# Output projection's input rings for its first blocks, and the down pass's residual adds on VectorE with later norms

## The chip, the cores and the metric

The kernel runs on one core of a Trainium2 chip. The metric is the device time of one execution in microseconds (us), the median over several runs. Five engines work side by side, each through its own instructions in order: TensorE (PE, matmuls), VectorE (DVE), ScalarE (ACT), GpSimd (POOL) and SyncE (SP), which here issues most of the DMAs. They wait for each other by semaphores.

## The reference

One layer of an encoder, with the same weights for a prompt of 2048 tokens and a sample of 256; d is 1024, the feed-forward width is 2816.

```python
h = rmsnorm(x, norm1_w)
p = h @ w_in
mq, mk, mv, mo, gates, aq, ak, av = jnp.split(p, cuts, axis=-1)
m_out = mlstm_mixer(mq, mk, mv, mo, gates, b_gates, mh_norm_w)
a_out = attention_mixer(aq, ak, av, q_norm_w, k_norm_w)
x = x + jnp.concatenate([m_out, a_out], axis=-1) @ w_out
h = rmsnorm(x, norm2_w)
u = centred_dwconv(h @ w_up, conv_w, conv_b)
a, g = jnp.split(u, 2, axis=-1)
x = x + (jax.nn.silu(g) * a) @ w_down
return rmsnorm(x, final_norm_w)
```

All of it is float32. The kernel splits each operand into a high and a low part of a shorter format, and makes a product from three matmuls (high by high, high by low, low by high).

## The kernel before, in words

The 2304 tokens are worked on as columns. The phases, in order: input projection and norm; gates; attention side by side with the mLSTM (`run_both`, L1689); the output projection, `phase_c` (L999), begun when the mLSTM is through and woven into the rest of the attention; the up projection with convolution and silu; the down pass, which ends with the residual and the final norm.

**Who orders the work.** A scheduler puts the instructions of every engine in order as the kernel is built. Only PE, from the end of the mLSTM to the end of the attention, follows the order in which the code is written (L1707). There `run_both` takes one piece of attention and one piece of the output projection in turn; a piece of the latter is a chunk of 12 matmuls (a `yield` in `mm`, L1048).

**The output projection.** It goes over 9 blocks of 256 tokens (BT), in the order 0 to 6, 8, 7; `n` is the place in that order and `b` the block. A block has 8 input tiles `cmx` (128 of the 1024 mixed channels each), read from `mix_d`, and one tile `cx` of the residual input x. `loads(n, b)` (L1020) brings them in: per tile a DMA on SP (L1031), the high part by a copy on ACT (L1032) and the low part by a subtraction on DVE (L1033); then x (L1036). The tiles of a block live in one of two rings with room for exactly one block each:

- `mx` (MXB = 8), in the pool `c_s`, which is opened when the mLSTM's own pools are closed: its memory is free only when the mLSTM is through;
- `nT` (NTB = 8), in the pool `m_n`, the ring in which the mLSTM had its own inputs: it is free as soon as the last mLSTM projection has been made, earlier than `mx`.

A block's loads are called at the start of the block before it (L1089), so they wait, if for anything, for the last user of their ring. A block needs 4 outputs `z` of 2 x 128 channels, 48 matmuls each (L1045, into `po`), then the residual (DVE, L1052), a store (L1054), squares (ACT, L1056) and their sum (POOL, L1058). The weights `wo` come in two halves; the first (k = 0, for z = 0 and 1) is loaded early, the second (k = 1) has its stage in the pool `c_s`; L111 is its DMA, L112 its copy on ACT, L114 its subtraction on DVE.

**The down pass.** Strassen-like: 7 products (`DOPS`), of which each is made for 3 column blocks `z` of 384 tokens (CG), each of these over 11 pairs `p` of channel blocks, with 12 matmuls (L1531) each. That is 21 groups of 132 matmuls, one behind the other on PE. Activations `te`/`tet` come in pieces (L1416 on SP) and are split by ACT and DVE (L1373, L1374), as the weights `we`/`wet` are. After a group, `update` adds its result to the accumulators `c00`, `c01`, `c10`, `c11` (L1541 and, for the product t3, L1543 on DVE).

What else belongs to the end of the layer is called from a table: `at(n, f)` runs f behind the matmuls of step n, where n counts pairs p over all groups. `resid` (L1433) loads a residual tile `xe` (L1436 on SP) and adds it to an accumulator (L1438: 128 partitions x 1536 elements, 12 times). `squares` (L1444, ACT) and `collect` (L1450, L1453, POOL) make the sum of squares `sm`. `norm` (L1455) sums that over partitions (three small matmuls in the code, L1461, six in the profile), adds eps (DVE, L1464), takes the power -1/2 (POOL, L1465), spreads the result to all partitions by PE (three more, L146, six in the profile), scales 8 slices on DVE (L1469) and stores them (L1471, SP). `xe` and `qe` share a ring of 2 buffers ("x"), so a residual's load can wait until the squares of another accumulator have been collected.

The first three norms (hf = 0, z = 0 to 2) fall into the products t3 and t1. After t3's update of block z come the adds for `c10` and `c01`, the squares of `c10`, their collection, and then the norm of that block.

Of the kernel before, what the change touches and what calls it, by code (L numbers as in the profile page):

```python
# [12 lines left out]
ALU = mybir.AluOpType  # L13
# [79 lines left out]
def f32(ap):  # L93
    return ap.bitcast(F32)
# [48 lines left out]
def rstd_rows(g, ps, r, n):  # L143

    for t in range(n // P):
        g.nc.tensor.matmul(ps[:, t * P:(t + 1) * P], r[:, t:t + 1].to_broadcast([P, P]), g.ident, start=True, stop=True)  # L146
    return ps[:, 0:n]
# [851 lines left out]
def phase_c(g, sn, sp, pp, wps):  # L999
# [3 lines left out]
    nc = g.nc  # L1003
# [17 lines left out]
    def loads(n, b):  # L1021
        mx = []
        x = sp.tile([P, NCC, BT], F32, tag="x", name=f"cx{b}", bufs=2)
        for z in range(4):
            for o in range(2):
                c = 2 * z + o
                if n % 2 == 0:
                    m = sp.tile([P, 2, BT], F32R, tag="mx", name=f"cmx{b}_{c}", bufs=MXB)
                else:
                    m = sn.tile([P, 2, BT], F32R, tag="nT", name=f"cmx{b}_{c}", bufs=NTB)  # L1030
                nc.sync.dma_start(f32(m[:, 1]), g.mix_d[b, :, c])  # L1031
                nc.scalar.activation(m[:, 0], f32(m[:, 1]), AF.Copy)  # L1032
                nc.vector.tensor_tensor(m[:, 1], f32(m[:, 1]), f32(m[:, 0]), ALU.subtract)  # L1033
                mx.append(m)
        for t in range(2):
            nc.sync.dma_start(x[:, :, t * P:(t + 1) * P], g.xT[2 * b + t])  # L1036
        return x, mx
# [41 lines left out]

    order = (*range(NB - 2), NB - 1, NB - 2)  # L1080
    nxt = loads(0, 0)
    yield None, C_LEAD
    prev = None
    for n, b in enumerate(order):
        x, mx = nxt
        for z in range(4):
            if z == 1 and n + 1 < NB:
                yield 2 * order[n + 1], C_MM
                nxt = loads(n + 1, order[n + 1])  # L1089
            po = pp.tile([P, 2, BT], F32, tag="po", name=f"po{b}_{z}")  # L1090
            for k, _ in enumerate(mm(b, z, mx, po)):
                if z == 1 and k == 0 and prev is not None:
                    tail_b(*prev)
                if z < 3 or k < 3:
                    yield None, C_MM
            if z == 0:
                if prev is not None:
                    prev = (*prev[0:2], *tail_a(*prev))
                acc = sp.tile([P, 2, BT], F32, tag="acc", name=f"cacc{b}", bufs=1)
            post(b, z, x, po, acc)  # L1100
            if (n, z) > (5, 0) and sums:

                n2_sums(g, sp, 0, sums.pop(0), tag="rn", bufs=2)
        prev = (b, x, acc)
# [69 lines left out]
def banks(g, pool, name):  # L1174

    k = g.nbank = g.nbank + 1
    return pool.tile([P, 2, 512], F32, tag=f"p{k % 2}", name=name, bufs=1)
# [167 lines left out]
def phase_e(g, tc, pd):  # L1345


    nc = g.nc
    h = D // 2
    G3 = TW // CG  # L1350
    with ExitStack() as st:
# [68 lines left out]
        def spans(hf, z):  # L1420

            r, c = [], z * CG
            while c < (z + 1) * CG:
                b, o = divmod(c, HB)
                n = min(HB - o, (z + 1) * CG - c)
                r.append((c - z * CG, n, b * BLK + hf * HB + o))
                c += n
            return r

        def C(o, hf):  # L1430
            return quad[o, hf]

        def resid(o, hf, z):  # L1433
            x = sy.tile([P, 4, h], F32, tag="x", name=f"xe{o}{hf}_{z}", bufs=2)[:, :, 0:CG]
            for c, n, t in spans(hf, z):
                nc.sync.dma_start(x[:, :, c:c + n], g.x1_d[:, 4 * o:4 * o + 4, t:t + n])  # L1436
            a = C(o, hf)[:, :, z * CG:(z + 1) * CG]
            nc.gpsimd.tensor_tensor(a, a, x, ALU.add)  # L1438

        done = set()  # L1440

        def squares(o, hf, z, ms=(0, 1, 2, 3)):
            q = sy.tile([P, 4, h], F32, tag="x", name=f"qe{o}{hf}_{z}_{ms[0]}", bufs=2)[:, 0:len(ms), 0:CG]
            nc.scalar.activation(q, C(o, hf)[:, ms[0]:ms[-1] + 1, z * CG:(z + 1) * CG], AF.Square, scale=1.0 / 32.0)  # L1444
            return [q[:, m] for m in range(len(ms))]

        def collect(hf, z, qs):
            if (hf, z) not in done:
                done.add((hf, z))
                nc.gpsimd.tensor_tensor(sms[hf, z], qs[0], qs[1], ALU.add)  # L1450
                qs = qs[2:]
            for q in qs:
                nc.gpsimd.tensor_tensor(sms[hf, z], sms[hf, z], q, ALU.add)  # L1453

        def norm(hf, z, extra=()):  # L1455
            ps = banks(g, pd[(g.nbank + 1) // 2 % 2], f"r{hf}_{z}")
            sqs = [sms[hf, z], *extra]
            k = CG // P
            for t in range(k):
                for i, sq in enumerate(sqs):  # L1460
                    nc.tensor.matmul(ps[:, 1, 2 * t:2 * t + 2], sq[:, t * P:(t + 1) * P], g.ones, start=i == 0,  # L1461
                                     stop=i == len(sqs) - 1)
            r = sy.tile([P, 4], F32, tag="rcol", name=f"rcol{hf}_{z}", bufs=2)[:, 0:k]
            nc.vector.tensor_scalar(r, ps[:, 1, 0:2 * k].rearrange("p (t o) -> p t o", o=2)[:, :, 0], EPS, None, ALU.add)  # L1464
            nc.gpsimd.tensor_tensor(r, r, g.mhalf[:, 0:k], ALU.pow)  # L1465
            r = rstd_rows(g, ps[:, 0], r, CG)
            for c in range(NCC):
                a = C(c // 4, hf)[:, c % 4, z * CG:(z + 1) * CG]
                nc.vector.scalar_tensor_tensor(a, a, g.fw[:, c:c + 1], r, ALU.mult, ALU.mult)  # L1469
                for c0, n, t in spans(hf, z):  # L1470
                    g.st.dma_start(g.yT[c, :, t:t + n], a[:, c0:c0 + n])  # L1471
# [23 lines left out]
        def at(n, f):  # L1495
            todo.setdefault(n, []).append(f)
# [9 lines left out]
        for z in range(G3):  # L1506
            e = 2 * SZ + z * NP
            at(e + 3, lambda z=z: resid(0, 0, z))
            at(e + 8, lambda z=z: collect(0, z, squares(0, 0, z)))
            e = 4 * SZ + (z + 1) * NP  # L1510
            at(e + 1, lambda z=z: resid(1, 0, z))
            at(e + 3, lambda z=z: resid(0, 1, z))
            at(e + 6, lambda z=z: collect(0, z, squares(1, 0, z)))
            at(e + 14, lambda z=z: norm(0, z))
            e = 5 * SZ + (z + 1) * NP
            at(e + 2, lambda z=z: resid(1, 1, z))
            at(e + 8, lambda z=z: collect(1, z, squares(1, 1, z)))
            e = 6 * SZ + (z + 1) * NP
            if z < G3 - 1:
                at(e + 1, lambda z=z: collect(1, z, squares(0, 1, z)))  # L1520
                at(e + 8, lambda z=z: norm(1, z))
        for i, k in enumerate(DOPS):
            for z in range(G3):
# [20 lines left out]
                n = (i * G3 + z) * NP  # L1544
# [29 lines left out]
def body(tc, aps, phases="abcd"):  # L1574
# [5 lines left out]
    with ExitStack() as st:  # L1580
# [81 lines left out]
        with ExitStack() as s2:  # L1662
# [18 lines left out]
            pd.append(pool(s5, "d_v", bufs=1, space=PSUM))  # L1681
            phase_u(g, tc, s1, pd, ops, first)
        phase_e(g, tc, pd)
        for n in list(aps):
            if n.startswith("dbg_"):
# [91 lines left out]
```

## Time and profile before

| | us |
|---|---|
| median of 3 runs (3388.86, 3392.04, 3394.19) | 3392.04 |
| the profiled execution | 3394.19 |
| its span, first to last instruction | 3392.5 |
| PE busy | 3276.5 |
| DVE busy | 2426.0 |
| ACT busy | 1779.7 |
| POOL busy | 1360.6 |

The output projection's first matmul is at 1456.50, the first norm of the down pass (L1461) at 3206.24, the last row of PE at 3383.18. The mean granted clock of PE is 0.985 of full speed. Where PE is without work for a while, its matmuls run at a clock of about 0.5 for some us. A row of a timeline gives start, duration, engine, line, operation, output and input, shape and count, and in brackets how long the engine had been idle and what ended that.

### The profile page before, as it was taken

The numbers are of one execution on the slowest core, as the hardware profiler recorded it, in microseconds if no ns is written. First come the engines' busy times: TensorE is split into PE (matmuls) and PEld (weight loads), VectorE is DVE, ScalarE is ACT, GpSimd is POOL, SyncE is SP. The second block draws the span as 40 slices with busy tenths as digits, with TensorE's granted clock in tenths as the row PEclk, the third lists the DMA queues.
The fourth block names the chain that finished last, engine by engine and source line by source line (L and its number), as shares of the span: only waits on it lengthen the run. The fifth ranks groups of instructions, "written<-read, shape, count | busy, mean of one in ns | idle before, by whom it ended". The sixth has DMA issues, their size and how long they took to land. (4 is left out here: it accounts for less than half of the span.)

```text
span 3392.5 us, 57175 instructions
## 1 busy us (share of the span) xinstructions
PE 3276.5 (97%) x21402; PEld 3049.5 (90%) x21402; DVE 2426.0 (72%) x3759; ACT 1779.7 (52%) x3708; POOL 1360.6 (40%) x1684
## 2 busy tenths in 40 slices
PE   7989999999999999889999999999999999999998
PEld 6778888888888888778889999999999998999998
DVE  6875687777768878966765778878877776544464
ACT  4535666667766776655553544445555555323231
POOL 6544122213232232211245457744544442762332
PEclk9999999999999999999999999999999999999999
DMA  6766243333345444433347324425322223875463
GB/s 221 239 199 171 89 136 95 109 109 117 93 130 169 121 139 136 121 97 96 99 140 263 123 97 151 133 90 183 99 99 93 93 99 124 297 256 174 148 224 107
DMA packets 300262, 481.86 MB, mean 142 GB/s; under 512 B 36528, under 2 KB 186192, under 8 KB 299984
## 3 DMA queue, kind: packets, MB, share of 16 engines
q1 hardware_dynamic: 247600, 348.33, 32.5%
q0 software_dynamic: 35824, 120.42, 10.8%
q10 hardware_dynamic: 16560, 9.44, 0.9%
q8 instruction: 169, 2.77, 0.3%
q14 instruction: 109, 0.89, 0.1%
HBM read 336.19 MB, written 141.90 MB: 141 GB/s over the span
## 5 line engine op out<-in xcount | busy, mean ns | idle before, releaser
L605 DVE TENSOR_TENSOR pl<-ps,ph 128x512 fp32r<-128x512 f32 x520 | 352.6, 683 | 185.1 <-ACT ps L604 179.2
L1202 PE MATMUL pa<-nt,wut 128*128 128x290 f32 (+1 forms) x3168 | 448.9, 298 | 10.1 <-ACT u L1220 8.0
L1202 PEld LDWEIGHTS pa<-nt,wut 128*128 128x128 f32 x3168 | 433.1, 190 | 12.1 <-ACT u L1220 9.4
L603 ACT ACTIVATE ph<-ps 128x512 fp32r<-128x512 f32 x520 | 309.4, 595 | 252.2 <-PE ps L600 241.8
L574 DVE TENSOR_REDUCE mx<-px 128x1 f32<-128x512 f32 (+1 forms) x528 | 345.3, 670 | 76.1 <-PE px L573 74.1
L1312 DVE SCALAR_TENSOR_TENSOR y<-u,cw,y 128x1152 f32<-128x1152 f32 (+1 forms) x176 | 323.8, 1840 | 36.1 <-ACT yc L1310 17.3
L617 PE MATMUL pv<-ph,v 128*128 128x512 f32 (+1 forms) x1040 | 319.0, 400 | 0.6 <-ACT ph L603 0.3
L604 ACT ACTIVATE ps<-ps 128x512 f32<-128x512 f32 x520 | 310.3, 597 | 0.0
L1531 PE MATMUL et<-tet,wet 128*128 128x384 f32 x1584 | 281.1, 338 | 1.3 <-DVE tet L1374 0.7
L1531 PEld LDWEIGHTS et<-tet,wet 128*128 128x128 f32 x1584 | 278.7, 189 | 1.9 <-DVE tet L1374 1.1
L1045 PEld LDWEIGHTS po<-cmx,wo 128*128 128x128 f32 x1728 | 222.0, 192 | 19.3 <-ACT cmx L1032 11.4
L1045 PE MATMUL po<-cmx,wo 128*128 128x256 f32 x1728 | 226.4, 285 | 11.4 <-ACT cmx L1032 11.2
L1531 PE MATMUL e<-te,we 128*128 128x384 f32 x1188 | 212.5, 339 | 11.0 <-ACT te L1373 7.1
L1531 PEld LDWEIGHTS e<-te,we 128*128 128x128 f32 x1188 | 210.0, 190 | 12.1 <-ACT te L1373 7.3
L599 PE MATMUL ps<-qq,kk 128*128 128x512 f32 x520 | 215.5, 416 | 3.7 <-DVE mx L574 2.2
L600 PE MATMUL ps<-qm,kl 65*128 65x512 f32 x520 | 206.9, 400 | 0.0
L573 PE MATMUL px<-kk,qq 128*128 128x512 f32 (+1 forms) x528 | 202.1, 412 | 4.9 <-DVE mx L574 2.9
L763 PE MATMUL mj<-mn,wm 128*128 128x256 f32 x1296 | 202.1, 287 | 3.2 <-ACT og L777 1.9
L763 PEld LDWEIGHTS mj<-mn,wm 128*128 128x128 f32 x1296 | 185.8, 191 | 20.6 <-ACT og L777 2.0
L773 PEld LDWEIGHTS mv<-wm,mn 128*128 128x128 f32 x1296 | 184.1, 191 | 18.5 <-ACT qb L769 2.5
L773 PE MATMUL mv<-wm,mn 128*128 128x256 f32 x1296 | 197.8, 286 | 1.0 <-ACT qb L769 0.9
L617 PEld LDWEIGHTS pv<-ph,v 128*128 128x128 f32 (+1 forms) x1040 | 157.1, 163 | 37.3 <-ACT ph L603 1.8
(305 smaller groups left out, 7292.4 us busy)
## 6 DMA issues: line engine op xcount, KB each, us to landing
mn<-n_d SPq DMA_DIRECT2D x216, 256.0 KB, 3.2
ru<-w_up SPq DMA_DIRECT2D x88, 512.0 KB, 3.6
a_d<-y POOLq DMA_DIRECT2D x88, 288.0 KB, 2.6
a_d<-tc POOLq DMA_DIRECT2D x66, 288.0 KB, 3.1
n_d<-n1T SPq DMA_DIRECT2D x18, 1024.0 KB, 5.6
dm<-nm_d POOLq DMA_DIRECT2D x72, 256.0 KB, 4.0
mjn<-n_d SPq DMA_DIRECT2D x72, 256.0 KB, 3.1
mvn<-n_d SPq DMA_DIRECT2D x72, 256.0 KB, 3.2
```

The source lines that it names most:

```text
L574: nc.vector.tensor_reduce(s.mx[:, t, z0:z0 + 1], ps[:, 0:w], AX.X, ALU.max)
L599: nc.tensor.matmul(ps, kk[:, kc:kc + P], s.qq[:, 0:N], start=True, stop=False)
L603: nc.scalar.activation(ph, ps, AF.Exp)
L604: nc.scalar.activation(ps, ps, AF.Exp)
L605: nc.vector.tensor_tensor(pl, ps, f32(ph), ALU.subtract)
L617: nc.tensor.matmul(s.pv[0:HD if k in (1, 3) else P, 0:N], v, p, start=(kp == 0 and k == 0), stop=(2 * kp + 2 == s.nk and k == 5))
L763: nc.tensor.matmul(pj[:, o], s.w[c][:, a, o * P:(o + 1) * P], nT[c][:, :, h, :], start=(c + o + k == 0), stop=(c == NCC - 1 and k == 2 and ...
L773: nc.tensor.matmul(pv[:, o], nT[c][:, o, a, :], s.w[c][:, h, 256:512], start=(c + o + k == 0), stop=(c == NCC - 1 and k == 2 and o == 1))
L1045: nc.tensor.matmul(po[:, o], wo[z // 2][c][:, a, n], mx[c][:, h, :], start=(c == 0 and k == 0), stop=(c == NCC - 1 and k == 2))
L1202: nc.tensor.matmul(p[:, z], w[:, aa, c, :], ops[k][:, c, bb, z * m:z * m + m], start=c == 0 and i == 0 and not add, stop=c == NCC // 2 - 1 ...
L1312: nc.vector.scalar_tensor_tensor(y[:, s:e], u[:, s + k:e + k], cw[:, k, jj:jj + 1], y[:, s:e], ALU.mult, ALU.add)
L1531: nc.tensor.matmul(ps[m // 2][:, m % 2], w[:, aa, m * P:(m + 1) * P], t[:, bb], start=p == 0 and n == 0, stop=p == NP - 1 and n == 2)
```

## The change

Three edits.

1. In `loads`, block 0 takes its tiles from `nT` instead of `mx`, and block 1 from `mx` instead of `nT`. The others stay: even places in `mx`, odd ones in `nT`. So `mx` now holds blocks 1, 2, 4, 6 and the block at place 8, and `nT` holds 0, 3, 5, 7.
2. The residual add L1438 goes from GpSimd to VectorE.
3. The first three norms are called 2 steps, that is 24 matmuls, later.

```diff
@@ loads @@
-                if n % 2 == 0:
+                if n and (n == 1 or n % 2 == 0):
                     m = sp.tile([P, 2, BT], F32R, tag="mx", name=f"cmx{b}_{c}", bufs=MXB)
                 else:
                     m = sn.tile([P, 2, BT], F32R, tag="nT", name=f"cmx{b}_{c}", bufs=NTB)
@@ resid @@
             a = C(o, hf)[:, :, z * CG:(z + 1) * CG]
-            nc.gpsimd.tensor_tensor(a, a, x, ALU.add)
+            nc.vector.tensor_tensor(a, a, x, ALU.add)
@@ the table @@
             at(e + 6, lambda z=z: collect(0, z, squares(1, 0, z)))
-            at(e + 14, lambda z=z: norm(0, z))
+            at(e + 16, lambda z=z: norm(0, z))
```

What follows are the orders of the two kernels, before and after, where they differ. First SP's queue at the end of the attention, from the second half of the weights on (`cmx1_0` is block 1's first tile, `bq33` and `bq34` are queries of the attention, `x1_d` and `n2_d` results):

```order
-L1031 DMA cmx0_6_18610<-mix_d_64 128x256
-L1031 DMA cmx0_7_18614<-mix_d_64 128x256
+L1031 DMA cmx1_0_18920<-mix_d_64 128x256
+L1031 DMA cmx1_1_18924<-mix_d_64 128x256
...
+L1031 DMA cmx3_7_20070<-mix_d_64 128x256
+L1054 DMA x1_d_65<-cx0_18585 128x4x256
+L542 DMA bq33_19827<-q_d_113 128x2x128 x2
+L1070 DMA n2_d0_61<-cx0_18585 128x4x256 x2
+L1036 DMA cx2_19485<-xT 128x8x128 x2
+L1054 DMA x1_d_65<-cx1_18919 128x4x256
+L542 DMA bq34_20324<-q_d_113 128x2x128 x2
 L1031 DMA cmx2_0_19486<-mix_d_64 128x256
```

Behind the weights, block 0's loads have made room for block 1's; block 0's stand in the early place that block 1's had. Block 3's come in the place where block 2's were, and block 2's move behind the stores of blocks 0 and 1, to the place that block 3's had.

On DVE in the down pass, behind the update of t3's column block 1 (`tet1_0_0` is a piece of activations of the next product, `wet1_3` a weight of it), before:

```order
L1543 TENSOR_TENSOR c10_33652<-c10_33652,c11_33653 128x2x384 x2
L1374 TENSOR_TENSOR wet1_2_36237<-dwt1_2_36238,wet1_2_36237 128x512
L1374 TENSOR_TENSOR tet1_0_0_36327<-tet1_0_0_36327 128x1536
L1374 TENSOR_TENSOR wet1_3_36254<-dwt1_3_36255,wet1_3_36254 128x512
L1374 TENSOR_TENSOR wet1_4_36275<-dwt1_4_36276,wet1_4_36275 128x512
L1464 TENSOR_SCALAR rcol0_0_36301<-r0_0_36297 128x3
```

And after:

```order
L1543 TENSOR_TENSOR c10_33652<-c10_33652,c11_33653 128x2x384 x2
L1438 TENSOR_TENSOR c01_33650<-c01_33650,xe01_1_36297 128x4x384
L1374 TENSOR_TENSOR wet1_2_36237<-dwt1_2_36238,wet1_2_36237 128x512
L1438 TENSOR_TENSOR c10_33652<-c10_33652,xe10_1_36259 128x4x384
L1374 TENSOR_TENSOR tet1_0_0_36301<-tet1_0_0_36301 128x1536
L1374 TENSOR_TENSOR wet1_3_36254<-dwt1_3_36255,wet1_3_36254 128x512
L1374 TENSOR_TENSOR wet1_4_36275<-dwt1_4_36276,wet1_4_36275 128x512
L1374 TENSOR_TENSOR wet1_5_36292<-dwt1_5_36293,wet1_5_36292 128x512
L1374 TENSOR_TENSOR wet1_6_36317<-dwt1_6_36318,wet1_6_36317 128x512
L1464 TENSOR_SCALAR rcol0_0_36343<-r0_0_36339 128x3
```

Two adds of block 1 now stand in DVE's order ahead of the splits and of the norm's L1464 for block 0, and two more weight splits stand ahead of L1464.

On PE, the first of these norms (`r0_0`) among the matmuls of t3's last group, before:

```order
L1531 MATMUL et3_2_1_36220<-tet3_2_0_36117,wet3_3_35739 128x384 x6
L1461 MATMUL r0_0_36297<-ones_127,sm00_33659 128x2 x3
L1531 MATMUL et3_2_0_36219<-tet3_2_1_36175,wet3_4_35756 128x384 x6
L1531 MATMUL et3_2_1_36220<-tet3_2_1_36175,wet3_4_35756 128x384 x6
L1531 MATMUL et3_2_0_36219<-tet3_2_1_36175,wet3_5_35773 128x384 x6
L1531 MATMUL et3_2_1_36220<-tet3_2_1_36175,wet3_5_35773 128x384 x6
L1531 MATMUL et3_2_0_36219<-tet3_2_1_36175,wet3_6_35794 128x384 x2
L146 MATMUL r0_0_36297<-ident_118,rcol0_0_36301 128x128 x3
```

And after:

```order
L1531 MATMUL et3_2_1_36220<-tet3_2_1_36175,wet3_5_35773 128x384 x6
L1461 MATMUL r0_0_36339<-ones_127,sm00_33659 128x2 x3
L1531 MATMUL et3_2_0_36219<-tet3_2_1_36175,wet3_6_35794 128x384 x6
L1531 MATMUL et3_2_1_36220<-tet3_2_1_36175,wet3_6_35794 128x384 x6
L1531 MATMUL et3_2_0_36219<-tet3_2_1_36175,wet3_7_35811 128x384 x6
L1531 MATMUL et3_2_1_36220<-tet3_2_1_36175,wet3_7_35811 128x384 x6
L1531 MATMUL et3_2_0_36219<-tet3_2_2_36221,wet3_8_35828 128x384 x2
L146 MATMUL r0_0_36339<-ident_118,rcol0_0_36343 128x128 x3
```

Both steps of the norm, the sum over partitions and the spreading, stand 24 matmuls further on; between them lie 26 matmuls as before. The same holds for the other two norms, in the next product's groups. On POOL the 12 adds are gone, and the four collecting adds of block 1 now come ahead of the power of block 0's norm (L1465), behind which they came before. On SP the residual loads of t3's blocks come one piece of activations earlier. PE's order in the output projection is the same in both.

## The prediction, made before the result was known

> **What bounds the kernel now.** I read the page first, then what TensorE (PE) waits for, then the two places where the change works. The page says that PE is busy nearly all the time, so only PE's waits, and the half clock behind them, can be won.
>
> ```profile
> PE 3276.5 (97%) x21402; PEld 3049.5 (90%) x21402; DVE 2426.0 (72%) x3759; ACT 1779.7 (52%) x3708; POOL 1360.6 (40%) x1684
> ```
>
> PE's waits, grouped by the line that waits and the line that ends it (us in total, times, longest), have these two at the head:
>
> ```profile
> PE po L1045 <- ACT cmx L1032: 11.2, 1, 11.2
> PE r L146 <- POOL rcol L1465: 9.1, 3, 7.5
> ```
>
> The first is one wait at the start of the output projection, the second is mostly one norm of the down pass. The timeline of PE at the first (start, duration, operation, count, idle before and its releaser), and a window of it with the granted clock (PEclk, the column behind the busy times):
>
> ```profile
> 1456.50 0.58 PE L1045 MATMUL po<-cmx,wo 128*128 128x256 f32 x1 [11.22 <-ACT cmx L1032]
> 1457.25 2.71 PE L1045 MATMUL po<-cmx,wo 128*128 128x256 f32 x11 [0.17 <-DVE cmx L1033]
> ```
>
> ```profile
> 1457.00:1460.00 3.00, 2.83 (x13) 2.75 (x13) 2.54 (x8) 1.73 (x6) 0.00 (x0) 0.51 0.88 259
> ```
>
> So the wait costs 11.22 us and is followed by matmuls at half clock (0.51). What it waits for is on SP's queue and on ACT:
>
> ```profile
> 1392.74 2.93 SPq L1031 DMA_DIRECT2D cmx<-mix_d  x4
> ```
>
> ```profile
> 1450.18 5.64 SPq L1031 DMA_DIRECT2D cmx<-mix_d  x8
> ```
>
> ```profile
> 1454.20 1.94 ACT L112 ACTIVATE wo<-ro 128x512 fp32r<-128x512 f32 x3 [0.82 <-DMA ro<-w_out]
> 1456.05 2.69 ACT L1032 ACTIVATE cmx<-cmx 128x256 fp32r<-128x256 f32 x8
> ```
>
> The early group, at 1392.74, is block 1, in the ring nT; block 0, which PE needs first, is in mx, loaded at 1450.18 and copied on ACT behind the second half of the weights.
>
> The second place, on PE, and the clock behind it:
>
> ```profile
> 3195.73 10.68 PE L1531 MATMUL et<-tet,wet 128*128 128x384 f32 x60
> 3206.24 0.72 PE L1461 MATMUL r<-ones,sm 128*128 128x2 f32 x6
> ...
> 3219.12 1.65 PE L146 MATMUL r<-ident,rcol 128*128 128x128 f32 x6 [7.54 <-POOL rcol L1465]
> ```
>
> ```profile
> 3219.10:3225.00 5.90, 5.88 (x21) 5.88 (x22) 1.21 (x1) 2.52 (x3) 3.94 (x4) 0.53 1.05 364
> ```
>
> From 3195.73 to 3206.24 PE issues 60 matmuls, 0.175 us each. Who makes the row L146 late is seen on POOL, ACT and DVE:
>
> ```profile
> 3188.84 5.68 POOL L1453 TENSOR_TENSOR sm<-sm,qe 128x384 f32<-128x384 f32 x4 [1.60 <-ACT qe L1444]
> 3205.99 4.15 POOL L1438 TENSOR_TENSOR c<-c,xe 128x1536 f32<-128x1536 f32 x1 [11.47 <-DVE c L1541]
> 3211.04 3.80 POOL L1438 TENSOR_TENSOR c<-c,xe 128x1536 f32<-128x1536 f32 x1 [0.90 <-DVE c L1543]
> 3217.81 1.26 POOL L1465 TENSOR_TENSOR rcol<-rcol,mhalf 128x3 f32<-128x3 f32 x1 [2.97 <-DVE rcol L1464]
> ```
>
> ```profile
> 3214.87 1.48 ACT L1444 ACTIVATE qe<-c 128x1536 f32<-128x1536 f32 x1 [7.79 <-POOL c L1438]
> ```
>
> ```profile
> 3217.58 0.15 DVE L1464 TENSOR_SCALAR rcol<-r 128x3 f32<-128x3 f32 x1
> ```
>
> The two residual adds (L1438) of column block 1 hold POOL to 3214.84; ACT, in order, waits 7.79 us with them for its squares, the weight copies behind the squares are late, DVE's splits of those too, and L1464, which belongs to the norm of block 0, stands behind these splits on DVE.
>
> **Edit 1, the rings.** Block 0 takes the early slot: its last DMA is issued before 1400 (it began at 1392.74), and a load lands in 11.5 us at the longest (row below), so it is there before PE comes. PE cannot start at once: its bank is that of the last mLSTM product, which DVE reads here:
>
> ```profile
> 1445.31 0.29 DVE L935 TENSOR_TENSOR mmx<-mT,ogT 128x128 f32<-128x128 f32 x1 [0.42 <-PE mT L930]
> ```
>
> PE had been idle since 1456.50 − 11.22 = 1445.28, and now starts at about 1445.65: 10.85 us won. The wait of 0.17 goes. The first 12 matmuls took 0.58 + 2.71 = 3.29 us; 24 at full clock take 3.02 (row below), so 12 take 1.51: about 1.7 us won with the half clock. Together 12.7.
>
> Three things are given back. (a) The copies at 1454.20 and 1456.05 (8 weights at 0.65 and 8 inputs, 7.9 us) no longer lie under an idle PE but among the attention's. On ACT and on PE before:
>
> ```profile
> 1467.81 0.60 ACT L561 ACTIVATE qq<-pq 128x512 fp32r<-128x512 f32 x1 [1.14 <-PE pq L559]
> ```
>
> ```profile
> 1470.05 0.63 PE L573 MATMUL px<-kk,qq 128*128 128x512 f32 x2
> ```
>
> PE's product at 1470.05 comes 12.7 earlier, at 1457.4. The copy that it needs now stands behind the last weights and one cmx on ACT. The weights' copies end at 1456.1 as their data land; with 0.4 for the cmx and 0.6 for the copy itself it is ready at 1457.1 if attention's four other copies fit into ACT's idle gaps, and some 2 us later if they don't. I take 1458.6, a wait of 1.2, and 0.8 for the next few: 2.0, from 0 to 4.
>
> (b) Blocks 1 and 2 are now neighbours in mx, so block 2's loads wait for block 1's last matmul and are needed at once. This slot held block 3 before. PE, SP, ACT, DVE there, and how long such loads take to land:
>
> ```profile
> 1558.58 3.02 PE L1045 MATMUL po<-cmx,wo 128*128 128x256 f32 x24
> ```
>
> ```profile
> 1556.85 4.05 SPq L1031 DMA_DIRECT2D cmx<-mix_d  x8
> ```
>
> ```profile
> 1559.85 1.05 ACT L1032 ACTIVATE cmx<-cmx 128x256 fp32r<-128x256 f32 x3
> ```
>
> ```profile
> 1561.54 1.75 DVE L1033 TENSOR_TENSOR cmx<-cmx 128x256 fp32r<-128x256 f32 x5
> ```
>
> ```profile
> DMA to landing us min/median/max: 2.3/2.9/11.5
> ```
>
> The 24 matmuls are 12 of block 1 and 12 of block 2, so block 2 begins at 1558.58 + 1.51 = 1560.1 and its first chunk ends at 1561.6. Its fourth tile is split on DVE at 1561.54 + 4 × 0.35 = 1562.9, so the chunk ends near 1563.5: 2.0 us late. If SP issues a load as soon as its tile is free and ACT and DVE take it first, the wait shrinks to 0.2; with a landing of 11.5 it becomes 1556.85 + 11.5 + 0.9 (copy and split) − 1560.1 = 9.2. Block 3's loads, which move ahead on SP to the slot that opens with block 0's end, are early by a whole block, and what they pass on the queue (stores, block 2's residual input) is needed later than they are.
>
> (c) In this wait PE is idle for some 2 us. Whether that halves the clock is told by two like waits in the phase behind:
>
> ```profile
> 1892.65 5.01 PE L1202 MATMUL pa<-nt,wut 128*128 128x290 f32 x24 [2.07 <-ACT u L1220]
> ```
>
> ```profile
> 1892.60:1896.00 3.40, 3.35 (x16) 3.35 (x17) 3.36 (x4) 1.17 (x2) 0.00 (x0) 0.63 0.02 5
> ```
>
> ```profile
> 2122.83 3.50 PE L1202 MATMUL pa<-nt,wut 128*128 128x290 f32 x24 [2.44 <-ACT u L1220]
> ```
>
> After 2.07 us the same 24 matmuls took 5.01 (clock 0.63 over the window), after 2.44 us 3.50. So it may cost 1.5 or nothing. Block 2's wait is made of small pieces on a PE that is kept short of work, and I take 1.5.
>
> Phase C: 12.7 − 2.0 − 2.0 − 1.5 = 7.2 us won.
>
> **Edits 2 and 3, the adds and the norm.** PE's wait of 7.54 goes, and the half clock: 5.90 × (1 − 0.53) = 2.8. Together 10.3. The new chain, first for block 0, with these durations:
>
> ```profile
> 3177.07 5.14 DVE L1543 TENSOR_TENSOR c<-c,c 128x768 f32<-128x768 f32 x2
> ```
>
> ```profile
> L1543 DVE TENSOR_TENSOR c<-c,c x6: 945/947/4274, 3177.1 to 3235.9; 128x768 f32<-128x768 f32 x6
> ```
>
> ```profile
> L1374 DVE TENSOR_TENSOR tet<-tet x36: 1348/1758/4990, 2996.5 to 3284.3; 128x1536 fp32r<-128x1536 f32 x24, 128x1152 fp32r<-128x1152 f32 x12
> ```
>
> DVE alone takes 0.95 for L1543 (min/median/max in ns), and 1.76 for two sources of 128x1536, which I take for an add; the 5.14 was beside a POOL add of the same time, which is gone. So DVE's 12 new adds cost 21 us and hand back much of it. From 3177.1: two L1543 (1.9), two adds (3.5), squares (1.48): 3184.0. POOL's four adds, 4.1 to 5.7, end by 3189.7, where they ended at 3194.5 before. They free the buffer for which SP's queue waits with the last piece of the activations behind:
>
> ```profile
> 3195.57 2.95 SPq L1416 DMA_DIRECT2D tet<-a_d  x2
> ```
>
> ```profile
> 3201.62 1.17 ACT L1373 ACTIVATE tet<-tet 128x1152 fp32r<-128x1152 f32 x1 [11.49 <-DMA tet<-a_d]
> ```
>
> ```profile
> 3204.10 1.81 DVE L1541 TENSOR_TENSOR c<-et,c 128x768 f32<-128x768 f32 x2
> ```
>
> It goes out at 3191.9 instead of 3195.57 and all that stands behind it on DVE, the updates of block 1 first (3204.10), starts 3.6 earlier, at 3200.5. Then 1.8, two L1543 1.9, an add 1.76, a weight split 0.7, an add 1.76 : 3208.3; squares to 3209.8; POOL's four adds to 3213.9 or 3215.5; L1464 on DVE is long done (tet and four weight splits behind the add: 3212.7), and POOL's power, 0.9, ends at 3214.8 to 3216.4. Row L146 stood at 3219.12 − 7.54 = 3211.58; e + 16 puts it 24 matmuls later, 24 × 0.175 = 4.2: 3215.8. So the stall is 0 to 0.6. At e + 14 it would be 3.2 to 4.8: that is what the shift is worth. If the activations were not earlier, everything is 3.6 later and the stall 2.6 to 4.2. I take 0 and 10.3 won; the two later norms move by the same 4.2 and have one block's work less ahead of them on POOL too. The norm's scalings (L1469) and stores follow 4.2 later; only the stores read what they write, and the banks that they hold are one of four pairs in turn, taken again by the group after next, over 23 us (132 × 0.175) on.
>
> Sum: 7.2 + 10.3 = 17.5 us. The profiled execution took 3394.19 (its span is 3392.5), the median of the three runs is 3392.04. The first becomes 3376.7, the median 3374.5, and I forecast for the median.
>
> **Rivals.**
> 1. *No half clock at block 2* (that is (c) at 0). For it: the row of 2122.83; against: that of 1892.65. The gain is 19.0, the time 3373.0. The Trainium skill, "TensorE: Matmul & The Clock Gate", Part 1 (The HAM clock gate), has the clock fall only after a whole idle window of about 3.4 us; by that rule this rival is the forecast, but the row of 1892.65 (2.07 us idle, clock 0.63) does not agree with it.
> 2. *Block 2's loads land late.* By the longest landing the wait in (b) is 9.2 instead of 2.0: 3381.7. For it: the 11.5; against: the median 2.9, and the first three copies at 1559.85, 3 us after the issue at 1556.85.
> 3. *The norm's power stays late*, because the chain on DVE is longer than I sum, or SP's x1 loads come late. The stall is as long as before, the 10.3 are lost: 3384.8. Against it: POOL's two adds (7.9 us) leave the chain and the norm moves by 4.2.
> 4. *Slower: DVE waits for x1.* DVE works in order. An add that waits for its load holds the splits of weights and activations behind it. POOL waited so here, with nothing urgent behind it:
>
> ```profile
> 3043.67 4.80 POOL L1438 TENSOR_TENSOR c<-c,xe 128x1536 f32<-128x1536 f32 x1 [11.25 <-DMA xe<-x_d]
> ```
>
> PE stalls once such a wait exceeds the time by which activations are split ahead of their use: the piece copied at 3201.62, split before the row of 3204.10, is used from the group's 96th matmul on, and the group began 48 matmuls before the row of 3206.24, so at 3206.24 + 48 × 0.175 = 3214.6: some 10 us. With three such places, each at 7.5 + 2.8 as in the row of 3219.12, this is 31 where 10.3 is lost now: 20.7 more, less 7.2 of phase C: 3405.5. Against it: the adds at 3205.99 and 3211.04 waited for DVE, not for a load.
> 5. *Neither place decides*: other waits take over and the time stays, 3392.
>
> **How the numbers follow.** Forecast 0.38, rival 1 0.35, rival 2 0.11, rival 3 0.08, rival 4 0.05, rival 5 0.03. A measurement can tell about 0.2%, 6.8 us, from no change. Rival 3's gain of 7.2 lies at that bound and is halved: faster 0.38 + 0.35 + 0.11 + 0.04 = 0.88, same 0.04 + 0.03 = 0.07, slower 0.05. The best sum (a 0, b 0.2, c 0) is 12.5 + 10.3 = 22.8: 3369.2, and the three runs lie up to 3.2 below their median, so I go down to 3367; upwards the range takes in rivals 2 and 3: 3385.
>
> **What would show it.** Right: the wait of 11.2 at L1045 is gone and the first po follows the last mLSTM product within 0.5 us; a wait of about 2 us on cmx stands at block 2's start; L146's longest wait is under 1.5 us, and DVE's L1438 takes about 1.8. Wrong: a longer wait at L1045 in block 2, waits of PE for tet or wet split on DVE, DVE idle at L1438 for xe, or L146 still waiting over 3 us.

## The result and the profile after

| | before | after |
|---|---|---|
| median, us | 3393.11 (4 runs, 3388.86 to 3394.47) | 3371.99 (4 runs, 3365.06 to 3375.60) |
| ratio | | 0.9937, 95% interval 0.9919 to 0.9956 |
| profiled execution, us | 3394.19 | 3373.21 |
| its span, us | 3392.5 | 3371.5 |

The kernel became faster by 21.1 us, or 0.6%; the forecast was 3374.5, 17.5 us less than the median known then. Two more sets of five runs gave 3372.87 against 3391.81 (18.9 us, ratio 0.9940, 0.9927 to 0.9952) and 3372.31 against 3390.56 (18.3 us, 0.9942, 0.9929 to 0.9954).

Of PE's waits after the change, grouped as before, these belong to the two places (us in total, times, longest):

```profile
PE r L146 <- POOL rcol L1465: 1.5, 2, 1.3
PE po L1045 <- DVE cmx L1033: 1.3, 1, 1.3
PE px L573 <- ACT qq L561: 0.9, 1, 0.9
PE po L1045 <- DVE mmx L935: 0.4, 1, 0.4
```

The wait of 11.2 on ACT's cmx is gone from the list, the 9.1 of L146 is 1.5 (of which 1.3 is the last norm's, which was there before), and three small ones have come: at block 2's start, at a copy of qq, and at the bank of the last mLSTM product. PE's timeline at the start of the output projection and at block 2:

```profile
1442.01 0.33 PE L930 MATMUL mT<-ident,hh 128*128 128x128 f32 x1
1442.72 1.69 PE L1045 MATMUL po<-cmx,wo 128*128 128x256 f32 x12 [0.38 <-DVE mmx L935]
1444.25 0.63 PE L573 MATMUL px<-kk,qq 128*128 128x512 f32 x2
...
1544.77 2.12 PE L1045 MATMUL po<-cmx,wo 128*128 128x256 f32 x13
1548.20 2.53 PE L1045 MATMUL po<-cmx,wo 128*128 128x256 f32 x11 [1.32 <-DVE cmx L1033]
```

The first chunk begins 0.71 us behind the last mLSTM product (11.56 before) and takes 1.69 us at a granted clock of 1.00, where it took 0.58 + 2.71 us with a wait of 0.17 between before. In block 2, one matmul runs, then PE waits 1.32 us for the low part of the first tile. On DVE, this is what stood ahead of it:

```profile
1545.94 1.28 DVE L605 TENSOR_TENSOR pl<-ps,ph 128x512 fp32r<-128x512 f32 x2
1547.14 0.68 DVE L1052 TENSOR_TENSOR cx<-po,cx 128x512 f32<-128x512 f32 x1
1547.73 3.85 DVE L1033 TENSOR_TENSOR cmx<-cmx 128x256 fp32r<-128x256 f32 x8
```

ACT had copied the first tile from 1546.04 on, so the tile had landed by then, and the wait is for DVE's turn. Whether earlier loads would have spared it is tried below (parity). In the down pass, PE, DVE and POOL at the first norm:

```profile
3198.80 0.72 PE L1461 MATMUL r<-ones,sm 128*128 128x2 f32 x6
3199.38 4.75 PE L1531 MATMUL et<-tet,wet 128*128 128x384 f32 x26
3204.42 0.93 PE L146 MATMUL r<-ident,rcol 128*128 128x128 f32 x6 [0.28 <-POOL rcol L1465]
```

```profile
3187.82 1.81 DVE L1541 TENSOR_TENSOR c<-et,c 128x768 f32<-128x768 f32 x2
3189.55 1.82 DVE L1543 TENSOR_TENSOR c<-c,c 128x768 f32<-128x768 f32 x2
3191.29 1.75 DVE L1438 TENSOR_TENSOR c<-c,xe 128x1536 f32<-128x1536 f32 x1
3192.96 0.69 DVE L1374 TENSOR_TENSOR wet<-dwt,wet 128x512 fp32r<-128x512 f32 x1
3193.56 1.75 DVE L1438 TENSOR_TENSOR c<-c,xe 128x1536 f32<-128x1536 f32 x1
```

```profile
3197.04 6.49 POOL L1453 TENSOR_TENSOR sm<-sm,qe 128x384 f32<-128x384 f32 x4 [20.51 <-ACT qe L1444]
3203.48 0.88 POOL L1465 TENSOR_TENSOR rcol<-rcol,mhalf 128x3 f32<-128x3 f32 x1
```

The chain runs as it was summed: two L1543 in 1.82 instead of 5.12, adds of 1.75, then POOL's four collecting adds and the power, which ends just when PE comes to L146. DVE's other work became shorter without POOL's adds beside it: the six L1543 took 12.2 us in all before and take 5.5, the splits L1374, 140 in all, took 201.5 and take 185.5. So the page's first line shows DVE no busier, though it took over 12 adds of 1.75 (21 us):

```profile
PE 3274.1 (97%) x21402; PEld 3047.9 (90%) x21402; DVE 2421.2 (72%) x3771; ACT 1779.4 (53%) x3708; POOL 1311.9 (39%) x1672
```

**Where the time came from.** In two executions the same program point can be compared. The last mLSTM product began at 1444.94 before and 1442.01 after: 2.9 us of the 21.0 between the spans lie ahead of the change. Two stretches hold the rest: C, from that product to the last L1045 (start to start), and D, from the first to the last L1531 of the products with transposed names (et). The row of D, before and then after (min/median/max ns, first and last start):

```profile
L1531 PE MATMUL et<-tet,wet x1584: 332/336/667, 3012.0 to 3305.5; 128*128 128x384 f32 x198
```

```profile
L1531 PE MATMUL et<-tet,wet x1584: 331/338/442, 2999.9 to 3282.9; 128*128 128x384 f32 x198
```

D took 293.5 and takes 283.0. C took 406.1 (1444.9 to 1851.0) and takes 397.1 (1442.0 to 1839.1). That is 10.5 + 9.0 = 19.5 of the remaining 18.1; the stretches between and behind gave 1.4 back. Single profiles of one kernel differ by some us in each stretch, so the averages further down weigh more than this pair.

### The profile page after: what moved, and what is told of

Read it like the earlier page. It is cut to its first block, busy times and chain, and to the rows that moved or that the text cites. A ratio compares the mean times of both kernels' runs of the same rounds, so it can differ in the third digit from the quotient of the medians.

```text
span 3371.5 us, 57154 instructions
## 1 busy us (share of the span) xinstructions
PE 3274.1 (97%) x21402; PEld 3047.9 (90%) x21402; DVE 2421.2 (72%) x3771; ACT 1779.4 (53%) x3708; POOL 1311.9 (39%) x1672
## 5 line engine op out<-in xcount | busy, mean ns | idle before, releaser
L605 DVE TENSOR_TENSOR pl<-ps,ph 128x512 fp32r<-128x512 f32 x520 | 353.3, 684 | 184.1 <-ACT ps L604 176.5
L1202 PE MATMUL pa<-nt,wut 128*128 128x290 f32 (+1 forms) x3168 | 448.3, 297 | 9.2 <-ACT u L1220 7.6
L1202 PEld LDWEIGHTS pa<-nt,wut 128*128 128x128 f32 x3168 | 432.4, 190 | 11.5 <-ACT u L1220 9.4
L1531 PE MATMUL et<-tet,wet 128*128 128x384 f32 x1584 | 279.2, 337 | 1.1 <-DVE tet L1374 1.1
L1531 PEld LDWEIGHTS et<-tet,wet 128*128 128x128 f32 x1584 | 276.9, 188 | 1.4 <-DVE tet L1374 1.4
L1045 PEld LDWEIGHTS po<-cmx,wo 128*128 128x128 f32 x1728 | 221.8, 192 | 10.0 <-DVE cmx L1033 1.5
L1045 PE MATMUL po<-cmx,wo 128*128 128x256 f32 x1728 | 226.3, 285 | 1.8 <-DVE cmx L1033 1.3
L1531 PE MATMUL e<-te,we 128*128 128x384 f32 x1188 | 212.9, 340 | 9.9 <-ACT te L1373 7.1
L1531 PEld LDWEIGHTS e<-te,we 128*128 128x128 f32 x1188 | 210.4, 190 | 11.0 <-ACT te L1373 7.3
```

What stands on the lines that cost most here:

```text
L605: nc.vector.tensor_tensor(pl, ps, f32(ph), ALU.subtract)
L1045: nc.tensor.matmul(po[:, o], wo[z // 2][c][:, a, n], mx[c][:, h, :], start=(c == 0 and k == 0), stop=(c == NCC - 1 and k == 2))
L1202: nc.tensor.matmul(p[:, z], w[:, aa, c, :], ops[k][:, c, bb, z * m:z * m + m], start=c == 0 and i == 0 and not add, stop=c == NCC // 2 - 1 ...
L1531: nc.tensor.matmul(ps[m // 2][:, m % 2], w[:, aa, m * P:(m + 1) * P], t[:, bb], start=p == 0 and n == 0, stop=p == NP - 1 and n == 2)
```

## The experiments

All runs, against the runs of the kernel before that were made beside them, with the two stretches of each profiled execution worked out in the same way:

| kernel | median, us | before, us | ratio (95%) | C, us | D, us |
|---|---|---|---|---|---|
| before | | | | 406.1 | 293.5 |
| rings_only | 3381.25 | 3391.84 | 0.9967 (0.9954 to 0.9979) | 397.6 | 295.2 |
| down_only | 3380.87 | 3391.84 | 0.9967 (0.9955 to 0.9980) | 403.2 | 286.0 |
| adds_only | 3382.53 | 3391.84 | 0.9970 (0.9960 to 0.9980) | 402.1 | 288.9 |
| norm_only | 3393.86 | 3391.84 | 1.0004 (0.9995 to 1.0013) | 404.6 | 294.5 |
| after (first) | 3371.99 | 3393.11 | 0.9937 (0.9919 to 0.9956) | 397.1 | 283.0 |
| after_again | 3372.87 | 3391.81 | 0.9940 (0.9927 to 0.9952) | 394.1 | 282.8 |
| after_third | 3372.31 | 3390.56 | 0.9942 (0.9929 to 0.9954) | 393.9 | 281.5 |
| parity | 3372.24 | 3391.81 | 0.9937 (0.9925 to 0.9950) | 397.4 | 281.4 |
| late_cross | 3376.68 | 3391.81 | 0.9953 (0.9940 to 0.9965) | 400.8 | 285.4 |
| adds_twice | 3368.92 | 3391.81 | 0.9931 (0.9918 to 0.9945) | 395.3 | 281.7 |
| norm12 | 3369.02 | 3393.08 | 0.9932 (0.9919 to 0.9944) | 394.1 | 282.8 |
| xe_thrice | 3376.00 | 3393.08 | 0.9947 (0.9933 to 0.9960) | 395.7 | 292.4 |
| parity_norm12 | 3370.01 | 3390.56 | 0.9937 (0.9924 to 0.9951) | 391.5 | 282.0 |

### The edits one by one

**rings_only**, the first edit alone:

```diff
-                if n % 2 == 0:
+                if n and (n == 1 or n % 2 == 0):
```

> Only the rings of blocks 0 and 1 are changed. Theory: the wait of 11.2 us at the first L1045 goes with its half clock, 12.6 us, and 3.7 come back (the qq copies behind the weights' on ACT, the wait at block 2's start and a half clock behind it), so 9 us less than before, about 3384; L146 still waits 7.5 us. Rival: the two places share a cause (all of DVE's and POOL's work shifts), so the rings alone bring much less than 9 or much more, and L146's wait changes too.

Measured: 10.6 us less, C shorter by 8.5, D within 2 us of before (L146 waits 7.1 us and, in the second norm, 2.8, where it waited 0.3 before). The theory holds for the output projection; whether the rings have to do with the second norm's wait, one profile cannot say.

**down_only**, the second and third edits alone:

```diff
-            nc.gpsimd.tensor_tensor(a, a, x, ALU.add)
+            nc.vector.tensor_tensor(a, a, x, ALU.add)
-            at(e + 14, lambda z=z: norm(0, z))
+            at(e + 16, lambda z=z: norm(0, z))
```

> Only the adds on VectorE and the later norms. Theory: L146's wait of 7.5 us and its half clock go, 9.4 to 10.3 us less than before, about 3383.5; the wait of 11.2 us at L1045 stays. Rival: VectorE's 12 new adds, 21 us in all, show on PE as waits for split weights or activations, and the gain is under 5 us.

Measured: 11.0 us less; L1045 waits 11.2 as before. D is 7.5 shorter in this profile, and the longest wait left in it is one of 2.0 for a piece of activations at 3033. The two gains, 10.6 and 11.0, make 21.6; the whole change gave 18.3 to 21.1. So the gains add up within what the runs can tell, and nothing shows that the two places touch each other.

**adds_only**, the second edit alone (L1438 on VectorE, norms at e + 14):

> Only the adds on VectorE, the norms where they were. Theory: the chain to the power on POOL ends as in the changed kernel, and L146 stands 24 matmuls, 4.2 us, earlier, so its first wait is 3.2 to 4.8 us with a half clock of about 2.5 behind it: the gain is 2 to 5 us, not 9.4. Rival: the shift of the norms is worth nothing, since the chain shortens with them; the first wait is under 1 us and the gain the whole 9.4.

Measured: 9.3 us less, so the theory falls, and the prediction's price of the later norms with it. PE and POOL at the first norm:

```profile
3205.54 0.72 PE L1461 MATMUL r<-ones,sm 128*128 128x2 f32 x6
3206.13 6.66 PE L1531 MATMUL et<-tet,wet 128*128 128x384 f32 x37
3212.62 0.92 PE L146 MATMUL r<-ident,rcol 128*128 128x128 f32 x6
```

```profile
3207.81 3.45 POOL L1453 TENSOR_TENSOR sm<-sm,qe 128x384 f32<-128x384 f32 x2 [20.45 <-ACT qe L1444]
3211.23 1.33 POOL L1465 TENSOR_TENSOR rcol<-rcol,mhalf 128x3 f32<-128x3 f32 x1
3212.54 2.08 POOL L1453 TENSOR_TENSOR sm<-sm,qe 128x384 f32<-128x384 f32 x2
```

L146 has no wait at all. It stands 37 matmuls behind L1461, not 26, and the power has moved between the collecting adds. The scheduler placed both anew once the chain on DVE was different. The wait that was expected here had been worked out with the changed kernel's order, which is not this kernel's. D is still 288.9, with other small waits (1.8 for a piece of activations, 1.1 and 0.6 for an update, 1.2 for the last of the three norms), of which single profiles cannot say what the e + 14 has to do with them.

**norm_only**, the third edit alone:

> Only the later norms, the adds stay on GpSimd. Theory: the chain over GpSimd's adds stays as long as it was, and L146 comes 4.2 us later to it: its first wait is 7.5 - 4.2 = 3.3 us, with the half clock still behind it, a gain of about 4 us. Rival: the shift is all that was needed, the wait falls under 1 us and the gain is over 8 us.

Measured: no gain, 1.0004 (0.9995 to 1.0013). Neither number held: L146 still waits 5.8 us, and 3.7 in the second norm. On DVE before the norm's L1464:

```profile
3211.52 4.88 DVE L1374 TENSOR_TENSOR wet<-dwt,wet 128x512 fp32r<-128x512 f32 x4
3216.32 0.15 DVE L1464 TENSOR_SCALAR rcol<-r 128x3 f32<-128x3 f32 x1
```

```profile
3217.49 1.65 PE L146 MATMUL r<-ident,rcol 128*128 128x128 f32 x6 [5.83 <-POOL rcol L1465]
```

With the norm called later, all four splits of weights stand ahead of L1464 where two of them did. The chain moved along with PE's row, 1.7 of the 7.5 was won, and the second norm lost more than that (3.7 where it waited 0.3). With adds_only beside it, which has no wait at this norm, it was GpSimd's adds that made the chain long.

### The norm's place, and VectorE's room

**norm12**, the changed kernel with the norms earlier still:

```diff
-            at(e + 16, lambda z=z: norm(0, z))
+            at(e + 12, lambda z=z: norm(0, z))
```

> The changed kernel with the three norms at e + 12, 48 matmuls earlier than in the change. Adds alone at e + 14 had no wait of L146 in the first norm, because the order of PE put L146 37 matmuls behind L1461 instead of 26, and on GpSimd the power stood ahead of two of the four collecting adds. Theory: the place of the call matters little, since the order is planned anew around it: L146's waits in the three norms stay under 2 us each, the time within 5 us of the changed kernel. Rival: the 4.2 us per 24 matmuls of the prediction holds, and at e + 12 the first norm waits 7 us or more, with the half clock 10 us and more slower.

Measured: D 282.8, as in the changed kernel, and 3369.02 us, not slower. The three norms:

```profile
3194.14 0.93 PE L146 MATMUL r<-ident,rcol 128*128 128x128 f32 x6 [0.50 <-POOL rcol L1465]
...
3220.34 0.83 PE L146 MATMUL r<-ident,rcol 128*128 128x128 f32 x6
...
3243.72 0.83 PE L146 MATMUL r<-ident,rcol 128*128 128x128 f32 x6
```

On POOL the power now precedes all four collecting adds of the next block (it took 4.13 us there, beside splits on DVE from 3189.79 to 3193.34; 0.88 in the changed kernel):

```profile
3189.95 4.13 POOL L1465 TENSOR_TENSOR rcol<-rcol,mhalf 128x3 f32<-128x3 f32 x1 [17.81 <-DVE rcol L1464]
3194.07 4.41 POOL L1453 TENSOR_TENSOR sm<-sm,qe 128x384 f32<-128x384 f32 x4
```

L146 stands 40 matmuls behind L1461 here. So with the adds on VectorE the call may stand at e + 12, 14 or 16: the scheduler sets the distance. No run shows the shift to be worth anything: adds_only and down_only, without it and with it, lie 1.7 us apart with intervals that overlap.

**adds_twice**, the changed kernel with each add made twice on VectorE, so that the residual counts double:

```diff
             nc.vector.tensor_tensor(a, a, x, ALU.add)
+            nc.vector.tensor_tensor(a, a, x, ALU.add)
```

> The changed kernel with each of the 12 residual adds made twice on VectorE (the residual counts double). Theory: VectorE has room; only the chain to the first norm is longer by two adds, 3.5 us, so L146's first wait grows from 0.3 to 3 to 4 us with a half clock of up to 2.5, 5 us at most of the 21 us of added work. Rival: VectorE bounds the down pass, and the time grows by 10 to 21 us, in waits of PE for split activations and weights.

Measured: 3368.92 us, not slower than the changed kernel, D 281.7, though DVE is busy 20 us longer:

```profile
PE 3271.4 (97%) x21402; PEld 3047.9 (91%) x21402; DVE 2441.4 (73%) x3783; ACT 1779.9 (53%) x3708; POOL 1312.8 (39%) x1672
```

VectorE has that much room in the down pass. L146 had no wait; it stood 38 matmuls behind the sums.

**xe_thrice**, the changed kernel with late residual tiles:

```diff
             for c, n, t in spans(hf, z):
-                nc.sync.dma_start(x[:, :, c:c + n], g.x1_d[:, 4 * o:4 * o + 4, t:t + n])
+                for _ in range(3):
+                    nc.sync.dma_start(x[:, :, c:c + n], g.x1_d[:, 4 * o:4 * o + 4, t:t + n])
```

> The changed kernel with every residual tile xe loaded three times over, one load behind the other, so that it arrives some 5 to 6 us later and SP's queue is held as long. Theory: VectorE's adds then wait for xe, but the splits behind them have some 10 us to spare: PE's waits in the down pass grow by under 3 us in all. Rival (the slower case of the prediction): the in-order wait on VectorE reaches PE, as waits for tet or wet split on VectorE or for the power, each with its half clock: 10 us and more slower.

Measured: 3376.00 us, 3 to 4 over the changed kernel, with intervals that overlap. The profiled execution was the slowest of the five: 3382.82, where the others took 3371.16 to 3376.83. DVE did wait for xe, and PE waited at one norm (waits of DVE, then PE's timeline):

```profile
DVE c L1439 <- DMA xe<-x_d: 11.2, 3, 5.0
```

```profile
3211.89 1.65 PE L146 MATMUL r<-ident,rcol 128*128 128x128 f32 x6 [4.43 <-POOL rcol L1466]
```

The one did not make the other. DVE's three waits ended at 3047.68, 3067.81 and 3229.02, and PE has no wait behind any of them. Ahead of the norm at 3211.89 stood these, on ACT and on POOL:

```profile
3193.51 1.17 ACT L1373 ACTIVATE tet<-tet 128x1152 fp32r<-128x1152 f32 x1 [10.13 <-DMA tet<-a_d]
```

```profile
3201.49 9.06 POOL L1454 TENSOR_TENSOR sm<-sm,qe 128x384 f32<-128x384 f32 x4 [21.66 <-ACT qe L1445]
```

SP issued this piece of activations at 3187.32, behind seven loads of xe that held its queue for 9.79 us; in the changed kernel ACT copied it at 3185.35. POOL's four adds then took 9.06 us, where they took 6.49. In this profile D is 10 us longer, by the norm's wait, one of 2.0 for activations (down_only and late_cross have like ones) and the half clock behind both. So the waits of PE grew by more than the 3 us expected, by way of SP's queue and the norm. That DVE's own wait for a load reaches PE, as the rival had it, isn't shown: waits of up to 5.0 us did not. In the changed kernel itself DVE's waits for xe are 2.3 us in all (2 times), and PE sees nothing of them.

### Block 2 and the rings

**parity**, the changed kernel with the rings in strict turn:

```diff
-                if n and (n == 1 or n % 2 == 0):
+                if n % 2:
```

> The changed kernel, with even places in the ring nT and odd ones in mx throughout: no two neighbours share a ring, the last block is in nT instead of mx. Theory: the wait of 1.3 us at block 2's start and the half clock behind it go, 2.5 to 3 us less in the output projection; what the last block costs in nT shows at the start of the up projection as later first loads, 0 to 5 us. Rival: the wait at block 2 is not of the ring but of VectorE's queue (two row maxima, two lows, a residual sum ahead of the splits), and it stays.

Measured: 3372.24 against 3372.87 beside it, no difference, where 2.5 to 3 us less were expected in the output projection. The wait at block 2 is gone:

```profile
1546.19 3.04 PE L1045 MATMUL po<-cmx,wo 128*128 128x256 f32 x24
```

So it was of the ring: earlier loads let DVE split earlier. But C is no shorter in this profile. A row maximum is later (first row below), behind a split (L1033) for which DVE waited 1.33 us; in parity_norm12, with the same rings, DVE has no such wait and PE's is 0.78. The second row is at the start of the up projection, where the cost of the last block was expected: a wait of 4.22 us (4.23 in parity_norm12, at most 2.6 in the three profiles of the changed kernel). The stretch between C and D is no longer for it, 1163.8 us where it is 1164.8 in after_again.

```profile
1462.73 0.79 PE L573 MATMUL px<-kk,qq 128*128 128x512 f32 x1 [2.19 <-DVE mx L574]
...
1856.82 5.34 PE L1202 MATMUL pc<-nt,wut 128*128 128x290 f32 x22 [4.22 <-DVE wut L1198]
```

**late_cross**, as parity, but the last block in mx:

```diff
-                if n and (n == 1 or n % 2 == 0):
+                if n % 2 or n == 8:
```

> As the one before, but the last block in mx, so that the last two share a ring. Theory: the wait moves from block 2's start to that of the last block and costs there what it cost before, 1 to 3 us: the time is that of the changed kernel within 1 us. Rival: less attention is left there, nothing fills the wait for a whole landing, and it costs over 5 us.

Measured: 3376.68, 3.8 us over the changed kernel beside it, with intervals that overlap. The wait moved to the last block, in three parts of 3.0 together:

```profile
1813.13 0.50 PE L1045 MATMUL po<-cmx,wo 128*128 128x256 f32 x2 [1.36 <-ACT cmx L1032]
...
1815.13 1.01 PE L1045 MATMUL po<-cmx,wo 128*128 128x256 f32 x3 [1.24 <-DVE cmx L1033]
...
1816.57 3.78 PE L1045 MATMUL po<-cmx,wo 128*128 128x256 f32 x16 [0.43 <-DVE cmx L1033]
```

With these waits and a half clock behind them, C in this profile is 5 us longer than the average with the change's rings. The time came out between the theory's 1 us and the rival's 5. The wait is longer here than the 1.32 at block 2, so block 2 looks like the better place; the runs' intervals don't show it, and the reason is open (PE had 4.8 us of the up projection's matmuls, L1202, from 1807.02 on while the loads were under way, so it was not without other work).

**after_again** and **after_third**, the changed kernel repeated:

> The changed kernel once more, on the chip of the three runs beside it. Theory: the parts add up, 9 us of the rings and 9.4 of the down pass, so 18 to 18.5 less than before, and the rest of the 21 seen at first is spread between executions. Rival: 21 again, so that about 3 us come from elsewhere.

> The changed kernel a third time, beside the run of both variants. Theory: the wait at block 2's start is 1.3 us again, and whether the clock is halved behind it varies from execution to execution: in the four executions with these rings so far it was halved once. Rival: the clock there is settled by the kernel, and the first execution's halving comes back.

Measured: 18.9 and 18.3 us less than before. Block 2's wait is 1.32 us in all seven executions with these rings (after three times, rings_only, adds_twice, norm12, xe_thrice). The granted clock (the column ahead of the last two) in the 4 us behind it, in the first execution of the changed kernel and in the third:

```profile
1548.20:1552.20 4.00, 4.00 (x16) 3.50 (x17) 3.94 (x8) 1.92 (x5) 2.15 (x2) 0.57 0.48 167
```

```profile
1548.95:1552.95 4.00, 4.00 (x23) 3.42 (x24) 3.60 (x8) 2.34 (x6) 1.82 (x2) 1.00 0.47 165
```

It was halved there in that first execution and in none of the other six (the expectation counts four executions so far; with norm12 and xe_thrice there were six). But in three of those (rings_only, after_again, norm12) it was halved behind the wait for qq instead, and in xe_thrice behind a row maximum. The wait and the clock in norm12:

```profile
1453.67 0.98 PE L573 MATMUL px<-kk,qq 128*128 128x512 f32 x2 [1.15 <-ACT qq L561]
```

```profile
1455.00:1458.00 3.00, 3.00 (x7) 2.17 (x8) 3.00 (x8) 3.00 (x9) 0.00 (x0) 0.51 1.16 305
```

So the theory holds, in that the kernel doesn't settle the place; one halving between the start of the output projection and 1560 came in five of the seven.

**parity_norm12**, both variants:

> The two variants that lost nothing, together: even places in nT and odd ones in mx, and the norms at e + 12. Theory: each took away waits of 1 to 3 us and gave others, so together they are the changed kernel within 4 us, with no wait on cmx at block 2's start. Rival: both gains are real and add up, over 4 us less than the changed kernel beside it.

Measured: 3370.01 against 3372.31 beside it, ratios 0.9937 and 0.9942 with intervals that overlap. It is the changed kernel within what can be told, with no wait on cmx at block 2.

## Why the prediction was right, point by point

- **Sum and sign.** 17.5 us were forecast. C, averaged over the four profiles with the old rings (404.0) and the seven with the change's (395.4), is 8.6 shorter, where 7.2 was summed. D, over the three with the adds on GpSimd (294.4) and the six with both down-pass edits and nothing else changed there (283.4), is 11.0 shorter, where 10.3 was summed. In neither stretch do the two groups overlap (402.1 to 406.1 against 393.9 to 397.6, 293.5 to 295.2 against 281.4 to 286.0). Together 19.6, and the three sets of runs gave 18.3 to 21.1.
- **The wait at L1045.** Right: 11.22 became 0.38, for the bank that DVE's L935 frees, and the first chunk runs at full clock. The start moved by 11.56 − 0.71 = 10.85 and the chunk with its wait of 0.17 is 3.46 − 1.69 = 1.77 shorter: 12.6 where 12.7 was forecast.
- **What comes back in C.** (a) was 2.0, from 0 to 4: measured 0.92 for qq, and row maxima at 1456.82 and 1462.75 that waited 0.30 and 0.77 where two waited 0.55 each before: 0.9. (b) was 2.0: measured 1.32. The ring made it, as summed (parity has none), but the tile itself was there in time for PE; DVE had two splits of the attention (L605) and the residual (L1052) first. (c) was taken at 1.5 at block 2: there it came once in seven, but a halving of that size came in five of seven, mostly behind the wait for qq of (a), where I had not looked for one. Not in the sum at all: near 1800 PE waits 1.7 to 3.5 us for the output projection's own norm (L146, rs_c) in ten of these eleven profiles, and a halved clock followed in six of the seven with the change's rings and in two of the four with the old ones, about 1 us more on average. So two of the three terms were too large and one loss was missing; that C came out so near is luck in part.
- **Rival 1, no half clock at block 2**, was the better one for the place; the 1.5 us were mostly paid elsewhere, so that its time, 3373.0, and the forecast, 3374.5, both stand near the measured 3372.0 to 3372.9. The runs don't tell them apart, and that the forecast kept a halving in its sum, for a place where it mostly did not come, is luck.
- **The chain of the norm.** Right in its steps and its end: DVE's update of block 1 came 4.6 us earlier against PE than before (3187.82 with PE's program shifted by 11.6, where 3.6 was forecast), POOL's power ended just as PE came to it, and the first norm's stall was 0 to 1.3 in the profiles with both edits (xe_thrice apart), where 0 to 0.6 was forecast. POOL's four adds took 6.5, more than the 4.1 to 5.7: the first of them took 3.22, beside splits on DVE. This and the earlier start cancel. The 3.6 has no row behind it; the sum's own ends of POOL's adds, 3194.5 and 3189.7, make 4.8.
- **The worth of the shift, wrong.** "At e + 14 it would be 3.2 to 4.8: that is what the shift is worth." That step held the changed kernel's order fixed and moved one row in it. adds_only had no wait there, norm12 0.5. The scheduler sets the distance between L1461 and L146 and the power's place on POOL for each source anew.
- **Rival 3 (a late power) and rival 4 (VectorE waiting for x1)** did not come. With later loads (xe_thrice) one profile has a late power, 4.43 us, as rival 3 has it, by way of SP's queue; rival 4's path, from a wait of DVE for x1 to PE, was not seen.
- **Not in the forecast:** 2.9 of the first profiled difference lay ahead of the change. Over the profiled executions of all kernels the last mLSTM product began at 1439.3 to 1444.9; the execution of before that the sum was made against is the latest of them.

## What to carry to other kernels

A ring's buffer is free when its last user is done, so it pays to ask which ring the first block of a new phase takes: here it was worth 8.6 us. The price is that two neighbours may then share a ring; here it was a wait of 1.3 us. Where a scheduler orders the engines, price an edit in the order that it makes: a row's place in one kernel says nothing of its place with one edit less. An engine that isn't the bottleneck can take over work for nothing if the order leaves it room: here 21 us of adds, and as much again in adds_twice, went to VectorE, which was 72% busy, and PE did not wait longer for it.

## What the runs showed of the hardware

- The same wait of 1.32 us, at the same point of the program, was followed by a half clock (0.57 over 4 us, some 1.7 us lost) in one of seven executions, and waits of 0.9 to 1.15 us for qq in three. In windows of 1 us from 1440 to 1859 and from 2985 to 3310, the halved stretches that end inside, in all 14 profiles, last 3.4 us or a whole multiple of it, so that one costs a busy PE 1.7 us or a multiple. Whether a short wait halves the clock cannot be read off from one profile. The Trainium skill ("TensorE: Matmul & The Clock Gate", Part 1: The HAM clock gate) asks for a whole idle window of about 3.4 us for it; these waits are shorter, so the runs don't agree with that, in the executions named.
- Beside a GpSimd add of 128x1536 (4.15 us), DVE's two L1543 took 5.12 us, and 1.82 without it. With L1543 and the splits L1374 shorter by 6.7 and 16.0 us in all, moving 12 adds (21.4 us) from GpSimd to VectorE left DVE's total where it was: 2426.0 before, 2421.2 after. GpSimd is slowed likewise: a collecting add of 128x384 took 3.22 us beside DVE's weight splits, where the median is 1.02.
- The last mLSTM product, which lies ahead of the change, began within 5.6 us over 14 profiled executions, over a quarter of the change's whole worth; why it varies is open. A profile's span alone is no measure of an effect of this size; the stretch around the change is.
